# Two pairs of 512-column projection blocks in place of four blocks of 256, with their weights loaded from ScalarE's queue

## The chip, the core and the metric

The kernel runs on one core of one Trainium2 chip. The metric is the device time of one execution in microseconds. Before the change it is 2110.87 us, the median of three runs (2110.83 to 2110.98).

## The reference

One encoder layer over two sequences, a prompt of 512 tokens and a sample of 1024, width 1024, all float32. What matters here is the first stage, one wide projection whose result is cut into parts:

```python
proj = jnp.einsum('btd,de->bte', u, w_in) + b_in        # u = rmsnorm(x) * g
(na_q, na_k, na_v, gla_q, gla_k, gla_v, gla_g, lr_fwd, lr_bwd,
 gate_na, gate_gla) = jnp.split(proj, split_points, axis=-1)
na_o  = neighbourhood_attention(na_q, na_k, na_v, na_rpb)
gla_o = gla_bidirectional(gla_q, gla_k, gla_v, log_a_fwd, log_a_bwd)
gla_o = rmsnorm(gla_o, gla_norm_g) * silu(gla_g)
merged = sigmoid(gate_na) * (na_o @ w_br_na) + sigmoid(gate_gla) * (gla_o @ w_br_gla)
```

`gla_v`, `gla_g` and `na_v` are 512 columns wide each. After it come a squared-ReLU MLP and norms.

## The kernel before

Every float32 product is made from two float32r parts: an operand is split into a high part (ScalarE copies it to float32r) and a low part (VectorE subtracts), and three matmuls add hi*hi, hi*lo and lo*hi. The norm writes `u_hi` and `u_lo`, with d_model on the partitions, into SBUF, and they stay there for the whole projection.

The projection consists of units. A `dense_cm` unit gives 128 output columns for 512 tokens: the weights are stationary, 512 tokens stream, 24 matmuls. A `dense_tm` unit (token-major, L255) gives 256 output columns for 128 tokens: the tokens are stationary and 256 weight columns stream (`tm_half`, L244 to 253), also 24 matmuls. `gla_v` (second half, block 1), `na_v` (blocks 2 and 3) and `gla_g` (blocks 4 and 5) are token-major, 12 units each, in the order 4, then three units of `k1`, then 1, 5, 2, 3. (Block 0 is made earlier, while the norm runs.) Units 10 and 11 of a block are interleaved so that the block's first half of weights is free early.

The weights come through `Ring` (L32): tiles of 128x1024 are loaded by SyncE's queue into two raw buffers, split into three rotating pairs of buffers, and `fill` is called where a unit begins.

The result of a unit lies in one of three PSUM banks `psd` and is evacuated when `run_dense` (L343) calls `flush`, about 1.2 us of matmul after the unit's end. `out_tm` (L313) does it for token-major units: VectorE adds the bias (L316) into `sv`, one of two buffers `st`. Then, for blocks 4 and 5, ScalarE does a SiLU, GpSimd multiplies, and SyncE's queue stores it to `glag_d`; for blocks 2 and 3, ScalarE and VectorE split it (L153, L154) into `svr` or `svl`, one buffer each, and two DMAs store it to `nv_d`; for block 1 it is stored to `glav_d`.

Beside the units runs a side chain, the gated linear attention (`gla_all`, L554): `run_dense` counts the cost that a unit yields (0.325 for three matmuls of 256 columns, 0.65 for three of 512), and each time the count passes 3.9 it lets the side chain issue its next step. The side chain goes through levels: VectorE makes Q and K of a level (L633, L637) and what the next level needs (L646 to L649), TensorE multiplies them (L622), VectorE merges the product into `att` (L660). A step on TensorE takes two levels. There are three segments per head pair: 0P, 0S (two halves), 1P, 1S. Each ends with `kd` (L672, L694), an update (L703) and, after the last half, a scan on VectorE (L715, L716) that the output matmuls (L726, L727) wait for. Every engine executes its instructions in the order in which they were issued, so side chain and evacuation share VectorE in that order.

Of the kernel before, what the change touches and what calls it, by code (L numbers as in the profile page):

```python
# [31 lines left out]
class Ring:  # L32


    def __init__(self, nc, raw, rawtag, nraw, pool, tag, nslots, items):
        self.nc, self.raw, self.pool, self.items = nc, raw, pool, items
        self.rawtag, self.tag, self.nraw, self.nslots = rawtag, tag, nraw, nslots
        self.loaded, self.parts = [], []

    def load(self):  # L40
        i = len(self.loaded)
        t = self.raw.tile([128, 1024], F32, tag=self.rawtag, bufs=self.nraw, name=f"{self.tag}r{i}")
        self.nc.sync.dma_start(t, self.items[i])
        self.loaded.append(t)

    def split(self):
        i = len(self.parts)
        t = self.loaded[i]
        hi = self.pool.tile([128, 1024], F32R, tag=self.tag + "h", bufs=self.nslots, name=f"{self.tag}h{i}")
        lo = self.pool.tile([128, 1024], F32R, tag=self.tag + "l", bufs=self.nslots, name=f"{self.tag}l{i}")  # L50
        self.nc.scalar.activation(hi, t, AF.Copy)  # L51
        self.nc.vector.tensor_tensor(lo, t, hi.bitcast(F32), op=ALU.subtract)  # L52
        self.parts.append((hi, lo))

    def fill(self, live):
# [10 lines left out]
    def step(self, live):

        if len(self.parts) < min(len(self.items), live + self.nslots):
            if len(self.loaded) == len(self.parts):
                self.load()  # L70
            self.split()
            if len(self.loaded) < len(self.items):
                self.load()

    def get(self, i):
        return self.parts[i]
# [3 lines left out]
def tile_trunk(ctx: ExitStack, tc: tile.TileContext, d: dict, y: bass.AP):  # L80
    nc = tc.nc
# [25 lines left out]
    rngp = rnge.enter_context(tc.tile_pool(name="rng", bufs=1))  # L107
# [22 lines left out]
    def add_mv(b):  # L130
        add(f"mv{b}", d["wmv"][2 * b], d["wmv"][2 * b + 1])

    for n in ("q0", "k0", "q1"):
        add(n, d["wst"][ST[n]])
    add_mv(4)
    add("k1", d["wst"][3])
    add_mv(1)
    add_mv(5)
    add_mv(2)
    add_mv(3)  # L140
# [8 lines left out]
    ring = Ring(nc, raw, "wraw", 2, rngp, "w", 3, items)  # L149
# [8 lines left out]
    zero = cst.tile([128, 128], F32, name="zero")  # L158
    V.memset(zero, 0.0)
# [95 lines left out]
    def dense_tm(b, i, evac):  # L255


        wi = where[f"mv{b}"]

        def mm():  # L260
            if i == 0:
                ring.fill(wi)
            if b not in brow:
                load_brow(b)
            if i == 6 and TM.index(b) < 5:
                load_brow(TM[TM.index(b) + 1])
# [11 lines left out]
        return mm  # L278

# [142 lines left out]
    def norm_side():  # L422
# [11 lines left out]
        gkw = p0.tile([128, 512], F32, name="gkw")  # L434
# [30 lines left out]
        for i in range(1, 12):  # L465
# [20 lines left out]
    ns = norm_side()  # L486
    warm = ps("b")
# [336 lines left out]

    mid = []
# [387 lines left out]
    def wout(g, hook):  # L1213

        mh, ml = m_[g]
        for n in range(2):
            for kq in range(4):
# [5 lines left out]
                for t in range(6):  # L1223
# [78 lines left out]
    uraw, uhl, useq = {}, {}, []  # L1302
# [23 lines left out]
    def u_step(m):  # L1326


        if 0 < m <= 224:
# [19 lines left out]
    def up_all(side):  # L1349
# [62 lines left out]
        for p in range(33):  # L1412
            cu, pv = dict(p=p, g=p // 16, j=p % 16) if p < 32 else None, cu
            for pos in range(7):
                u = pv if pos == P4 else cu
                if u:
# [7 lines left out]
                    for k in range(4):  # L1424
# [3 lines left out]
                        T.matmul(u[b], wl[:, es], c[:, 0, k], start=False, stop=(k == 3), skip_group_check=True)  # L1428
                    ev(pos)
# [337 lines left out]
def _layout(x_prompt, x_sample, norm_mix_g, w_in, b_in, na_rpb, gk_fwd_w, gk_fwd_b, gk_bwd_w, gk_bwd_b,  # L1767
# [21 lines left out]
    d["wmv"] = c(np.stack([stat(w[h * 512:(h + 1) * 512, m:m + 256]) for m in mv for h in range(2)]))  # L1789
# [74 lines left out]
```

## Time and profile before

| | |
|---|---|
| median of three runs | 2110.87 us |
| profiled execution, its own time | 2112.74 us |
| its span, first to last instruction | 2110.8 us |
| TensorE busy | 2089.7 us (99%) |
| VectorE busy | 1318.2 us (62%) |
| ScalarE busy | 974.9 us (46%) |
| 256-column matmuls of L250 to L252 | 1440 in five blocks, 114.9 to 358.3 us |

TensorE's busy share counts each matmul from its start to its modelled end, and matmuls overlap, so the spacing between the starts of two neighbours is what one costs. The table says where time is spent over the whole run; what bounds one stretch is read from that stretch.

### The profile page before, as it was taken

Reading aid. Unit: us, or ns where it says so; the run is one execution under the profiler, and the core shown is the slowest. Engines: PE = TensorE matmul, PEld = TensorE weight load, DVE = VectorE, ACT = ScalarE, POOL = GpSimd, SP = SyncE. Lnnn points to the kernel's source line nnn. Section 1 sums busy time; section 2 is a strip of 40 time slices with the busy share of each in tenths; the row PEclk is TensorE's granted clock in tenths of the full one; section 3 lists DMA queues with packets and bytes.
Section 4 is the critical chain, followed back from the end, with each engine's and each line's share of the span. In section 5 each row is a group of like instructions: output and inputs, shape, how many; then the busy total and the mean of one; then the engine's idle time right before and its main releaser. Section 6 shows DMA issues by size and latency. Waiting matters only on the chain.

```text
span 2110.8 us, 32043 instructions
## 1 busy us (share of the span) xinstructions
PE 2089.7 (99%) x11964; PEld 1890.3 (90%) x11964; DVE 1318.2 (62%) x2428; ACT 974.9 (46%) x1914; POOL 64.5 (3%) x92
## 2 busy tenths in 40 slices
PE   9999999999999999999999999999999999999998
PEld 8899998888888888898898999999999888888887
DVE  7465875767346666465576777997887444443544
ACT  6532232333345555452353666676666333333442
POOL 1020100000000000000000000000000000000000
PEclk9999999999999999999999999999999999999999
DMA  6342334564386776466666566766876755454643
GB/s 212 116 147 86 97 112 140 126 170 91 111 246 202 217 217 198 149 212 226 245 215 250 174 165 173 228 202 197 267 234 176 264 200 186 157 170 162 220 170 110
DMA packets 256426, 381.86 MB, mean 181 GB/s; under 512 B 35856, under 2 KB 163856, under 8 KB 256272
## 3 DMA queue, kind: packets, MB, share of 16 engines
q1 hardware_dynamic: 256128, 379.56, 57.5%
q8 instruction: 94, 1.54, 0.3%
q14 instruction: 60, 0.49, 0.1%
q10 hardware_dynamic: 144, 0.26, 0.0%
HBM read 256.02 MB, written 123.73 MB: 180 GB/s over the span
## 4 chain that ended last, share of the span: by engine, by line
PE 80%; DVE 2%; ACT 1%; DMA 1%; issue 1%; SPq 0%; POOLq 0%; DVEq 0%; ACTq 0%
PE psd L225 6%; PE psd L227 6%; PE psd L226 6%; PE psa L1426 4%; PE psa L1428 4%; PE psa L1427 4%; PE psa L1581 2%; PE psa L1580 2%; PE psa L1582 2%; PE psb L1580 2%; PE psb L1581 2%; PE psb L1582 2%; PE psc L1581 2%; PE psc L1580 2%; PE psc L1582 2%; PE psb L1428 2%
## 5 line engine op out<-in xcount | busy, mean ns | idle before, releaser
L154 DVE TENSOR_TENSOR al<-al,ah 128x1024 fp32r<-128x1024 f32 x82 | 100.2, 1223 | 145.7 <-ACT ah L153 135.2
L153 ACT ACTIVATE ah<-al 128x1024 fp32r<-128x1024 f32 x82 | 86.6, 1057 | 225.2 <-DMA al<-ads 134.3
L225 PE MATMUL psd<-uhiS,wh 128*128 128x512 f32 x448 | 179.6, 401 | 0.8 <-ACT st L287 0.8
L227 PE MATMUL psd<-uhiS,wl 128*128 128x512 f32 x448 | 175.3, 391 | 0.0
L226 PE MATMUL psd<-uloS,wh 128*128 128x512 f32 x448 | 174.8, 390 | 0.0
L1426 PE MATMUL psa<-c,uwh 128*128 128x384 f32 x512 | 171.7, 335 | 0.8 <-DVE xb L1366 0.7
L1428 PE MATMUL psa<-c,uwl 128*128 128x384 f32 x512 | 171.0, 334 | 0.0
L1427 PE MATMUL psa<-c,uwh 128*128 128x384 f32 x512 | 171.0, 334 | 0.0
L1331 DVE TENSOR_TENSOR uwl<-ux,uwh 128x512 fp32r<-128x512 f32 x192 | 131.0, 687 | 58.7 <-ACT uwh L1347 57.6
L1347 ACT ACTIVATE uwh<-ux 128x512 fp32r<-128x512 f32 x192 | 120.0, 626 | 79.6 <-DVE ux L1341 66.3
L52 DVE TENSOR_TENSOR wl<-wr,wh 128x1024 fp32r<-128x1024 f32 x70 | 85.5, 1223 | 105.2 <-ACT wh L51 94.1
L51 ACT ACTIVATE wh<-wr 128x1024 fp32r<-128x1024 f32 x70 | 73.8, 1056 | 143.9 <-PE psc L1231 66.0
L225 PEld LDWEIGHTS psd<-uhiS,wh 128*128 128x128 f32 x448 | 84.2, 188 | 18.3 <-ACT st L287 1.2
L227 PEld LDWEIGHTS psd<-uhiS,wl 128*128 128x128 f32 x448 | 84.1, 188 | 18.2
L226 PEld LDWEIGHTS psd<-uloS,wh 128*128 128x128 f32 x448 | 84.3, 188 | 16.1
L1426 PEld LDWEIGHTS psa<-c,uwh 128*128 128x128 f32 x512 | 96.1, 188 | 1.5 <-DVE xb L1366 1.0
L1427 PEld LDWEIGHTS psa<-c,uwh 128*128 128x128 f32 x512 | 96.1, 188 | 0.0
L1428 PEld LDWEIGHTS psa<-c,uwl 128*128 128x128 f32 x512 | 96.1, 188 | 0.0
L250 PE MATMUL psd<-wh,uhiS 128*128 128x256 f32 x320 | 92.7, 290 | 0.8 <-DVE sv L316 0.8
L251 PE MATMUL psd<-wl,uhiS 128*128 128x256 f32 x320 | 90.9, 284 | 0.0
L252 PE MATMUL psd<-wh,uloS 128*128 128x256 f32 x320 | 90.8, 284 | 0.0
L225 PE MATMUL psd<-uhiP,wh 128*128 128x512 f32 x224 | 90.3, 403 | 0.0
(557 smaller groups left out, 5889.4 us busy)
## 6 DMA issues: line engine op xcount, KB each, us to landing
ux<-in_wup_dram SPq DMA_DIRECT2D x64, 512.0 KB
al<-ads SPq DMA_DIRECT2D x48, 512.0 KB
al<-ad SPq DMA_DIRECT2D x34, 512.0 KB
bq<-t_d SPq DMA_DIRECT2D x64, 256.0 KB
wr<-in_wst_dram SPq DMA_DIRECT2D x28, 512.0 KB
gate_d<-st SPq DMA_DIRECT2D x48, 256.0 KB
sg<-gate_d SPq DMA_DIRECT2D x32, 384.0 KB
ad<-xa SPq DMA_DIRECT2D x64, 192.0 KB
```

Source lines behind the costliest of these rows:

```text
L154: V.tensor_tensor(lo, src, hi.bitcast(F32), op=ALU.subtract)
L225: T.matmul(p, wh, xh[:, k, sl], start=(k == 0), stop=False)
L226: T.matmul(p, wh, xl[:, k, sl], start=False, stop=False)
L227: T.matmul(p, wl, xh[:, k, sl], start=False, stop=(k == 7))
L1331: V.tensor_tensor(lo, usrc.pop(m - 1), hi.bitcast(F32), op=ALU.subtract)
L1347: A.activation(uhl[m][0], usrc[m], AF.Copy)
L1426: T.matmul(u[b], wh[:, es], c[:, 0, k], start=(new and k == 0), stop=False, skip_group_check=True)
L1427: T.matmul(u[b], wh[:, es], c[:, 1, k], start=False, stop=False, skip_group_check=True)
L1428: T.matmul(u[b], wl[:, es], c[:, 0, k], start=False, stop=(k == 3), skip_group_check=True)
L1580: T.matmul(p, ah[:, jj], bh[:, cs], start=((new or last) and jj == 0), stop=False, skip_group_check=True)
L1581: T.matmul(p, ah[:, jj], bl[:, cs], start=False, stop=False, skip_group_check=True)
L1582: T.matmul(p, al[:, jj], bh[:, cs], start=False, stop=(kh == 1 and jj == 7), skip_group_check=True)
```

## The change

Blocks 4 and 5 become one pair, blocks 2 and 3 another. A unit of a pair (`dense_pair`) makes 512 columns for 128 tokens: 24 matmuls of 512 columns in place of 48 of 256. Its end evacuates both halves of the bank one after the other through the same `out_tm`. Units 0 and 1, and units 10 and 11, of a pair are interleaved. The order becomes `k1`, pair (4, 5), pair (2, 3), block 1. Units yield 0.68 per three matmuls.

The weights of a pair come as eight pieces of 128x512 from a new input array, loaded by `A.dma_start`, that is from ScalarE's queue, four of them in flight at the second pair and two at the first. A piece is split into one 128x1024 buffer, high half and low half. `Ring` has eight buffers without a fixed use and a free list. The first pair's pieces are split during `k1`, the second's during units 10 and 11 of the first pair and the first two units of its own. `pr` is a raw piece, `pw` a split one.

```diff
+    def alloc(self, dt, name):
+        s = self.free.pop(0)
+        return s, self.pool.tile([128, 1024], dt, tag=f"w{s}", name=name)
...
+    def pw_load(q, n=1, s=None):
...
+            if s is None:
+                t = stg2.tile([128, 512], F32, tag=("svr", "svl")[k % 2], bufs=1, name=f"pr{q}{k}")
...
+            A.dma_start(t, d["wpr"][q, k])
+    def pw_split(q):
...
+        s, x = ring.alloc(F32R, f"pw{q}{k}")
+        split_act(x[:, :512], x[:, 512:], t)
...
+    def pw_ahead(mm, q):
+        def run():
+            for n, cost in enumerate(mm()):
+                yield cost
+                if n % 4 == 3:
+                    pw_split(q)
+                    pw_load(q)
+    def dense_pair(q, i, evac, nxt=None):
+        def step(p, k, j):
+            x = pw[q]["parts"][k][1]
+            xh, xl = tok_ap(u_hi, k, j), tok_ap(u_lo, k, j)
+            T.matmul(p, xh, x[:, :512], start=(k == 0), stop=False)
+            T.matmul(p, xh, x[:, 512:], start=False, stop=False)
+            T.matmul(p, xl, x[:, :512], start=False, stop=(k == 7))
+        def end(p, j):
+            for e in range(2):
+                evac(p[:, e * 256:e * 256 + 256], PAIRS[q][e], j)
...
+            ii = (i, i + 1) if i in (0, 10) else (i,)
...
+                    step(p[j], k, j)
+                    yield 0.68
+                if i == 0:
+                    if k in (2, 4):
+                        pw_split(q)
...
+                if i == 10:
+                    ring.free.append(pw[q]["parts"][k][0])
+                    if nxt:
+                        nxt(k)
+    def next_pair(k):
+        if k == -1:
+            pw_load(1, 2)
+        elif k == 0:
+            pw_load(1, 2, 0)
+        elif k != 3:
+            pw_split(1)
+            if k in (1, 2, 6, 7):
+                pw_load(1)
+    def next_ring(k):
...
+        if k in (0, 1):
+            ring.load()
+        elif k in (5, 7):
+            ring.split()
-            r = stg2.tile([128, 4, 2, 64], F32R, tag=("svr", "svl")[i % 2], bufs=1, name=f"svr{uid[0]}")
+            r = stg2.tile([128, 4, 2, 64], F32R, tag=("svr", "svl")[(i + b) % 2], bufs=1, name=f"svr{uid[0]}")
...
-    mid += [dense_tm(4, i, out_tm) for i in range(12)]
-    for n_, dst, cb in (("k1", glak_d, 3),):
-        mid += [dense_cm(n_, seg, out_cm(dst, cb, 128, cb < 2)) for seg in range(3)]
-    for b in (1, 5, 2, 3):
-        mid += [dense_tm(b, i, out_tm) for i in range(12)]
+    pw_load(0, 2)
+    mid = [pw_ahead(dense_cm("k1", seg, out_cm(glak_d, 3, 128)), 0) for seg in range(3)]
+    for q, nxt in enumerate((next_pair, next_ring)):
+        mid += [dense_pair(q, i, out_tm, nxt) for i in (0, *range(2, 11))]
+    mid += [dense_tm(1, i, out_tm) for i in range(12)]
```

The rest of the diff moves the tile `zero` and `gkw` into buffers that are free later, gives the bias rows three buffers, and lets the MLP's first part take its buffers from the ring's free list. From the neighbourhood attention on, the order on every engine is the one of before.

The instructions move as follows. First VectorE in the sample's levels (0S). Before, in block 2, one evacuation (`sv` from `psd`, then `svr`) stands between two levels (Q, K, X, Y; `att0S` is the merge):

```order
L316 TENSOR_TENSOR sv_2968<-psd_2920,brow_2610 128x256
L154 TENSOR_TENSOR svr_2970<-sv_2968,svr_2970 128x4x64
L660 COPY_PREDICATED att0S<-msk,psa_2975 128x512
L660 COPY_PREDICATED att0S<-msk,psa_2976 128x512
L633 TENSOR_TENSOR Q0S_3015<-q0S_2332,Y0S_2334 128x2x32x8
L637 TENSOR_TENSOR K0S_3017<-k0S_2333,X0S_2769 128x2x32x8
L646 TENSOR_TENSOR X0S_2769<-X0S_2769,Y0S_2334 128x32x8
L647 TENSOR_TENSOR X0S_2769<-X0S_2769,Y0S_2334 128x32x8
L649 TENSOR_TENSOR Y0S_2334<-Y0S_2334 128x2x32x8
L316 TENSOR_TENSOR sv_3038<-psd_2964,brow_2610 128x256
L154 TENSOR_TENSOR svr_3040<-sv_3038,svr_3040 128x4x64
```

Now, at the end of the first two units of pair (2, 3), four evacuations stand in a row ahead of the merge and the next K:

```order
L405 TENSOR_TENSOR sv_2239<-psd_2104,brow_1742 128x256
L146 TENSOR_TENSOR svr_2241<-sv_2239,svr_2241 128x4x64
L405 TENSOR_TENSOR sv_2246<-psd_2104,brow_2190 128x256
L146 TENSOR_TENSOR svr_2248<-sv_2246,svr_2248 128x4x64
L405 TENSOR_TENSOR sv_2260<-psd_2140,brow_1742 128x256
L146 TENSOR_TENSOR svr_2262<-sv_2260,svr_2262 128x4x64
L405 TENSOR_TENSOR sv_2267<-psd_2140,brow_2190 128x256
L146 TENSOR_TENSOR svr_2269<-sv_2267,svr_2269 128x4x64
L752 COPY_PREDICATED att0S<-msk,psa_2208 128x512
L752 COPY_PREDICATED att0S<-msk,psa_2209 128x512
L725 TENSOR_TENSOR Q0S_2285<-q0S_1394,Y0S_1396 128x2x4x64
L729 TENSOR_TENSOR K0S_2287<-k0S_1395,X0S_1705 128x2x4x64
```

Four evacuations, each a sum and a split, stand where there was one, and K of the level behind them comes after all four.

Second VectorE in the prompt's levels (0P). Before, in block 4, single evacuations stand between merges and levels:

```order
L316 TENSOR_TENSOR sv_1493<-psd_1443,brow_436 128x256
L660 COPY_PREDICATED att0P<-msk,psa_1429 128x512
L660 COPY_PREDICATED att0P<-msk,psa_1430 128x512
L316 TENSOR_TENSOR sv_1526<-psd_1480,brow_436 128x256
L633 TENSOR_TENSOR Q0P_1531<-q0P_1263,Y0P_1265 128x2x64x4
L637 TENSOR_TENSOR K0P_1533<-k0P_1264,X0P_1408 128x2x64x4
L646 TENSOR_TENSOR X0P_1408<-X0P_1408,Y0P_1265 128x64x4
L647 TENSOR_TENSOR X0P_1408<-X0P_1408,Y0P_1265 128x64x4
L649 TENSOR_TENSOR Y0P_1265<-Y0P_1265 128x2x64x4
L660 COPY_PREDICATED att0P<-msk,psa_1556 128x512
L660 COPY_PREDICATED att0P<-msk,psa_1557 128x512
```

Now the first two units of pair (4, 5) are evacuated in one go, four times into the two buffers `st`:

```order
L729 TENSOR_TENSOR K0P_1467<-k0P_1232,X0P_1326 128x2x32x8
L738 TENSOR_TENSOR X0P_1326<-X0P_1326,Y0P_1233 128x32x8
L739 TENSOR_TENSOR X0P_1326<-X0P_1326,Y0P_1233 128x32x8
L741 TENSOR_TENSOR Y0P_1233<-Y0P_1233 128x2x32x8
L405 TENSOR_TENSOR sv_1475<-psd_1364,brow_433 128x256
L405 TENSOR_TENSOR sv_1480<-psd_1364,brow_435 128x256
L405 TENSOR_TENSOR sv_1492<-psd_1371,brow_433 128x256
L405 TENSOR_TENSOR sv_1497<-psd_1371,brow_435 128x256
L752 COPY_PREDICATED att0P<-msk,psa_1444 128x512
L752 COPY_PREDICATED att0P<-msk,psa_1445 128x512
L725 TENSOR_TENSOR Q0P_1513<-q0P_1231,Y0P_1233 128x2x16x16
L729 TENSOR_TENSOR K0P_1515<-k0P_1232,X0P_1326 128x2x16x16
```

The third `sv` takes the buffer of the first, whose path through ScalarE, GpSimd and the store must have ended; the next Q and K stand behind it.

Third ScalarE at the change from the first pair to the second. Before, at the start of block 5, its queue holds two splits and then SiLUs:

```order
L51 ACTIVATE wh_2308<-wr_1716 128x1024
L51 ACTIVATE wh_2350<-wr_1890 128x1024
L332 ACTIVATE sv_2395<-sv_2395 128x256
L332 ACTIVATE sv_2463<-sv_2463 128x256
L332 ACTIVATE sv_2492<-sv_2492 128x256
L332 ACTIVATE sv_2523<-sv_2523 128x256
L332 ACTIVATE sv_2591<-sv_2591 128x256
L332 ACTIVATE sv_2622<-sv_2622 128x256
```

Now, in units 10 and 11 of pair (4, 5), DMA issues stand between the splits:

```order
L282 DMA pr_1974<-in_wpr_dram 128x512 x2
L145 ACTIVATE pw_1983<-pr_1897 128x512
L282 DMA pr_1986<-in_wpr_dram 128x512
L145 ACTIVATE pw_2020<-pr_1899 128x512
L282 DMA pr_2023<-in_wpr_dram 128x512
L145 ACTIVATE pw_2044<-pr_1974 128x512
L145 ACTIVATE pw_2062<-pr_1974 128x512
L145 ACTIVATE pw_2078<-pr_1986 128x512
L282 DMA pr_2081<-in_wpr_dram 128x512
L421 ACTIVATE sv_2089<-sv_2089 128x256
L421 ACTIVATE sv_2094<-sv_2094 128x256
```

Each DMA that reuses a raw buffer waits in ScalarE's queue until VectorE has made the low part from it.

## Rows read from the trace of the kernel before

**Rows 1.** Page, part 1: busy us (share) xinstructions of each engine.

```profile
PE 2089.7 (99%) x11964; PEld 1890.3 (90%) x11964; DVE 1318.2 (62%) x2428; ACT 974.9 (46%) x1914; POOL 64.5 (3%) x92
```

**Rows 2.** Stretches: PE, PEld, DVE, ACT, POOL busy us, granted clock, DMA share, GB/s.

```profile
115.00:211.00 96.00, 95.92 (x785) 91.17 (x785) 55.62 (x110) 25.40 (x61) 14.56 (x18) 1.00 0.35 115
211.00:331.00 120.00, 114.09 (x1031) 109.99 (x1027) 97.86 (x192) 32.60 (x72) 11.01 (x12) 1.00 0.33 106
...
140.00:150.00 10.00, 10.00 (x99) 9.75 (x98) 9.86 (x19) 1.40 (x4) 3.28 (x3) 1.00 0.45 145
...
330.00:340.00 10.00, 8.81 (x60) 8.67 (x61) 3.38 (x9) 2.61 (x11) 0.81 (x1) 0.83 0.27 79
```

**Rows 3.** Timeline of TensorE, token-major units: start us, duration us, line, tiles.

```profile
120.18 0.28 PE L250 MATMUL psd<-wh,uhiP 128*128 128x256 f32 x1
120.30 0.28 PE L251 MATMUL psd<-wl,uhiP 128*128 128x256 f32 x1
```

**Rows 4.** Timeline of TensorE, column-major units of 512.

```profile
71.05 0.39 PE L226 MATMUL psd<-uloS,wh 128*128 128x512 f32 x1
...
71.73 0.39 PE L226 MATMUL psd<-uloS,wh 128*128 128x512 f32 x1
```

**Rows 5.** Waits of TensorE, 100 to 700 us: total, times, longest.

```profile
PE psa L727 <- DVE stt0S L716: 2.6, 1, 2.6
PE psa L622 <- DVE K0S L637: 1.8, 2, 1.1
```

**Rows 6.** Timeline of TensorE, the side chain's steps that begin and end segment 0S.

```profile
210.23 0.50 PE L611 MATMUL psa<-qkh,two 64*128 64x512 f32 x2
...
242.24 2.06 PE L622 MATMUL psa<-Q0S,K0S 64*128 64x128 f32 x32
...
331.19 0.46 PE L727 MATMUL psa<-stt0S,qd0S 128*128 128x128 f32 x2 [2.58 <-DVE stt0S L716]
```

**Rows 7.** Timeline of VectorE in block 2: evacuation, merge, level, evacuation.

```profile
282.41 0.42 DVE L316 TENSOR_TENSOR sv<-psd,brow 128x256 f32<-128x256 f32 x1
283.36 0.43 DVE L154 TENSOR_TENSOR svr<-sv,svr 128x256 fp32r<-128x256 f32 x1 [0.53 <-ACT svr L153]
283.70 1.35 DVE L660 COPY_PREDICATED att0S<-msk,psa 128x512 f32<-128x512 uint8 x2
...
287.05 0.69 DVE L649 TENSOR_TENSOR Y0S<-Y0S 128x512 f32<-128x512 f32 x1
287.66 0.42 DVE L316 TENSOR_TENSOR sv<-psd,brow 128x256 f32<-128x256 f32 x1
```

**Rows 8.** Groups of VectorE, 211 to 332 us: busy, mean ns | idle before, releasers.

```profile
L316 DVE TENSOR_TENSOR sv<-psd,brow 128x256 f32<-128x256 f32 x31 | 13.0, 419 | 3.5 <-PE psd L252 2.5 <-POOL sv L334 0.9
...
L52 DVE TENSOR_TENSOR wl<-wr,wh 128x1024 fp32r<-128x1024 f32 x6 | 7.3, 1222 | 2.4 <-ACT wh L51 2.4
L154 DVE TENSOR_TENSOR svr<-sv,svr 128x256 fp32r<-128x256 f32 x16 | 6.8, 426 | 9.7 <-ACT svr L153 9.7
...
L154 DVE TENSOR_TENSOR qkl<-qk,qkh 128x512 fp32r<-128x512 f32 x2 | 1.4, 693 | 4.6 <-ACT qkh L153 4.6
```

**Rows 9.** Waits that a store's buffer ended, 100 to 480 us.

```profile
DVE sv L316 <- DMA glag_d<-sv: 7.3, 2, 3.8
...
ACT svr L153 <- DMA nv_d<-svr: 4.4, 1, 4.4
```

**Rows 10.** SyncE's queue: two stores.

```profile
109.32 0.80 SPq L541 DMA_DIRECT2D la_d<-zz  x2
...
120.79 0.32 SPq L335 DMA_DIRECT2D glag_d<-sv  x1
```

**Rows 11.** Timeline of VectorE: the instructions that waited for these stores; the start of 0P.

```profile
112.16 1.41 DVE L531 TENSOR_SCALAR zz<-psa,gkb 128x512 f32<-128x512 f32 x2 [2.56 <-DMA la_d<-zz]
...
124.99 0.42 DVE L316 TENSOR_TENSOR sv<-psd,brow 128x256 f32<-128x256 f32 x1 [3.47 <-DMA glag_d<-sv]
...
130.14 0.68 DVE L597 TENSOR_TENSOR qk<-q0P,k0P 128x512 f32<-128x512 f32 x1
```

**Rows 12.** Timeline of ScalarE: the split of 128x512.

```profile
130.85 0.63 ACT L153 ACTIVATE qkh<-qk 128x512 fp32r<-128x512 f32 x1 [0.18 <-DVE qk L597]
```

More of the change, by code (lines that the diff above doesn't have):

```diff
@@ L64, in fill @@
                 return
[L66 to L73, printed above, removed]
     def get(self, i):
-        return self.parts[i]
+        return self.parts[i][2:]
 @with_exitstack
@@ L128, in add @@
         items.extend(aps)
-    def add_mv(b):
-        add(f"mv{b}", d["wmv"][2 * b], d["wmv"][2 * b + 1])
-    for n in ("q0", "k0", "q1"):
+    for n in ("q0", "k0", "q1", "k1"):
         add(n, d["wst"][ST[n]])
[L135 to L140, printed above, removed]
+    add("mv1", d["wmv"][0], d["wmv"][1])
     for i in range(8):
@@ L148, in tile_trunk @@
         add(f"out{g}", *[d["wout"][i] for i in range(8)])
-    ring = Ring(nc, raw, "wraw", 2, rngp, "w", 3, items)
+    ring = Ring(nc, raw, 8, items)
+    ring.limit = where["mv1"]
     def split_act(hi, lo, src):
@@ L260, in mm @@
         def mm():
-            if i == 0:
+            if i == 4:
                 ring.fill(wi)
[L263 to L266, printed above, removed]
             if i == 11:
@@ L278, in dense_tm @@
         return mm
+    PAIRS = ((4, 5), (2, 3))
+    pw = [dict(n=0, raw=[], parts={}) for _ in PAIRS]
+    def pw_load(q, n=1, s=None):
+        w = pw[q]
+        if s is not None:
+            b, x = ring.alloc(F32, f"pr{q}{w['n']}")
+        for e in range(n):
+            k = w["n"]
+            if s is None:
+                t = stg2.tile([128, 512], F32, tag=("svr", "svl")[k % 2], bufs=1, name=f"pr{q}{k}")
+                w["raw"].append((t, None))
+            else:
+                t = x[:, e * 512:e * 512 + 512]
+                w["raw"].append((t, b if e == n - 1 else None))
+            A.dma_start(t, d["wpr"][q, k])
+            w["n"] += 1
@@ new lines, in pw_split @@
+    def pw_split(q):
+        w = pw[q]
+        k = len(w["parts"])
+        t, b = w["raw"].pop(0)
+        s, x = ring.alloc(F32R, f"pw{q}{k}")
+        split_act(x[:, :512], x[:, 512:], t)
+        w["parts"][k] = s, x
+        if b is not None:
+            ring.free.append(b)
+    def pw_ahead(mm, q):
[5 more added lines that the diff above has]
+                    pw_load(q)
+        return run
@@ new lines, in dense_pair, with mm @@
+    def dense_pair(q, i, evac, nxt=None):
[8 more added lines that the diff above has]
+                evac(p[:, e * 256:e * 256 + 256], PAIRS[q][e], j)
+        def mm():
+            if i == 0 and q == 0:
+                ring.release(where["k1"] + 1)
+            if i == 9 and nxt:
+                nxt(-1)
+            ii = (i, i + 1) if i in (0, 10) else (i,)
+            p = {}
+            for k in range(8):
+                for j in ii:
+                    if k == 0:
+                        if j == 1:
+                            flush()
+                        p[j] = ps("d")
+                    step(p[j], k, j)
+                    yield 0.68
+                    if k == 7:
+                        done.append(lambda j=j: end(p[j], j))
+                if i == 0:
+                    if k in (2, 4):
+                        pw_split(q)
+                    if k == 4:
+                        for b in PAIRS[q]:
+                            if b not in brow:
+                                load_brow(b)
+                if i == 6 and k == 0:
+                    load_brow(PAIRS[1][0] if q == 0 else 1)
+                if i == 10:
+                    ring.free.append(pw[q]["parts"][k][0])
+                    if nxt:
+                        nxt(k)
+        return mm
@@ L280, in out_cm @@
+    def next_pair(k):
[8 more added lines that the diff above has]
+    def next_ring(k):
+        ring.limit = len(items)
+        if k in (0, 1):
+            ring.load()
+        elif k in (5, 7):
+            ring.split()
+            if k == 7:
+                ring.load()
     def out_cm(dst, cb, row, scale=False):
@@ L433, in norm_side @@
         SP.dma_start(gkb, d["gkb"])
-        gkw = p0.tile([128, 512], F32, name="gkw")
         xn = {}
@@ L486, in tile_trunk @@
     ns = norm_side()
+    zero = p0.tile([128, 4, 32], F32, tag="lrt", bufs=4, name="zero").rearrange("p a b -> p (a b)")
+    V.memset(zero, 0.0)
     warm = ps("b")
@@ L1234, in wout @@
                         V.tensor_tensor(hs, acc[t], hs, op=ALU.add)
+                ring.release(wi + 1)
                 hook(n * 4 + kq)
@@ L1310, in u_load @@
             for e in es:
-                x = raw.tile([128, 1024], F32, tag="wraw", bufs=2, name=f"ux{p}{e}") if p % 2 == 0 else tmp(f"ux{p}{e}")
+                s, x = ring.alloc(F32, f"ux{p}{e}") if p % 2 == 0 else (None, tmp(f"ux{p}{e}"))
+                uslot.setdefault(p, []).append(s)
                 SP.dma_start(x, d["wup"][p % 16 * 2 + e])
@@ L1334, in u_step @@
                 uraw.pop(p)
+                ring.free += [s for s in uslot.pop(p) if s is not None]
                 u_load(p + 2)
@@ L1343, in u_step @@
             if m % 2 == 0:
-                uhl["t"] = [rngp.tile([128, 1024], F32R, tag=f"w{c}", bufs=3, name=f"uw{c}{m}") for c in "hl"]
+                uslot["w", m + 1], uhl["t"] = zip(*[ring.alloc(F32R, f"uw{c}{m}") for c in "hl"])
             sl = slice(m % 2 * 512, m % 2 * 512 + 512)
@@ L1428, in up_all @@
                         T.matmul(u[b], wl[:, es], c[:, 0, k], start=False, stop=(k == 3), skip_group_check=True)
+                    ring.free += uslot.pop(("w", n), ())
                     ev(pos)
```

43 lines of the change are left out of this document (22 added, 21 removed).

## The prediction

> **What bounds the kernel now.** I read the busy shares first: TensorE 99%, VectorE 62% [rows 1]. That makes TensorE the bound of the run, but the change touches only 115 to 358 us, so I read that stretch alone. There VectorE is busy for 55.6 of 96 us up to 211 us and for 97.9 of 120 us from there to 331 us, and in the second piece TensorE is idle for 120.0 - 114.1 = 5.9 us [rows 2]. The waits of TensorE say who ended that idle time: VectorE's scan (2.6 us) and the K of a level (1.8 us) are the largest [rows 5]. So in the sample's segment 0S, from its first matmuls at 210.23 us to the output matmul released at 331.19 us [rows 6], 121.0 us, TensorE and VectorE are close to a tie, and VectorE is a little late at the end. Elsewhere in the stretch TensorE waits for almost nothing.
>
> **What goes: half of 1152 matmuls.** Matmuls of 256 columns start 0.12 us apart [rows 3], those of 512 columns 0.227 us apart [rows 4] (0.68 us from one L226 to the next, three matmuls). Four blocks of 288 are 1152 x 0.120 = 138.2 us, two pairs of 288 are 576 x 0.2267 = 130.6 us: -7.7 us. The fixed part of a matmul, 2 x 0.120 - 0.2267 = 13 ns, is all there is to win.
>
> [...]
>
> **What is added on VectorE and ScalarE.** The four blocks' splits were 8 of 1.22 us on VectorE and become 16 of 128x512, for which `qkl` stands with 0.69 us [rows 8] (ScalarE 0.63 us each [rows 12]): +1.2 us on VectorE. Evacuations stay 48, each of 256 columns. What moves is where they stand. Before, the 24 that also split (blocks 2 and 3) lay beside the second half of 0S and its scan, and the first half of 0S lay beside blocks 1 and 5, whose evacuation is one instruction. Now pair (2, 3) lies beside nearly all of 0S.
>
> One such evacuation holds VectorE for 283.70 - 282.41 = 1.29 us, 0.53 of it idle for ScalarE; a level (merge to `Y`) holds it for 287.66 - 283.70 = 3.96 us [rows 7]. A TensorE step takes two levels. It costs TensorE 2.06 us [rows 6] and 7.8 us of counted dense cost: before 72 matmuls, 8.64 us, together 10.8; now 7.8 us of pair, together 9.96. VectorE needs 7.92 for the levels and 3.87 for three evacuations before, 11.8; now 7.8/5.44 x 2 x 1.29 = 3.7, so 11.6. VectorE was short by 1.0 us per step in block 2 and is short by 1.7 us in pair (2, 3), for five steps where there were three.
>
> **Sum over 0S.** VectorE's 120.8 us there contain evacuations and splits of dense weights: 15 plain sums at 0.34 (spacing), 16 with a split at 0.76 and their 9.7 us of waiting, six ring splits at 1.15 and 2.4 us, 3.5 us of other waits: 39.8 us [rows 8]. `qkl` waited 4.6 us, of which some 1.4 stays. The rest, 120.8 - 39.8 - 3.2 = 77.8 us, is the side chain. Counted in the new order between the same two points, VectorE has 7 piece splits (0.65 each), 5 plain sums, 24 sums with split at 1.29, 2 ring splits: 4.6 + 1.7 + 31.0 + 2.3 = 39.6 us. So 117.4 us if it never waits for a buffer.
>
> It will wait. In both interleaved unit pairs (0 and 1, 10 and 11) four evacuations become due within 0.7 us, and the third takes a buffer of the first two. For blocks 4 and 5 that is `st`: sum, SiLU, multiply, store; such waits were 3.8 and 3.5 us [rows 9]. For blocks 2 and 3 it is `svr`/`svl`, behind two stores; the one wait of that kind was 4.4 us [rows 9]. A store lands 112.16 - 110.12 = 2.0 us after its issue ended, or 124.99 - 121.11 = 3.9 us beside loads [rows 10, 11]. In 0S that hits three times (end of the first pair, start and end of the second): none to 3.3 us each, so 0 to 10 us; I take 6, 2 each, as `svr`'s DMAs start while the sums go on. VectorE then needs 123.4 us.
>
> TensorE's own work in the same piece: before 121.0 - 6.0 of waits = 115.0, of which 753 dense matmuls (counted in the order) are 90.4 and the side chain 24.6. Now 321 of pairs, 72.8, 78 of block 1, 9.4, and 24.6: 106.8. VectorE with 123.4 sets the end of the piece, with 123.4 - 121.0 = +2.4 us. Dense work that is no longer done inside it is done outside: the total falls by 7.7, the piece's own by 8.2, so the outside rises by 0.5.
>
> **The prompt's levels.** Two more waits come at the start of pair (4, 5). `qk` of 0P, made from 130.14 us before [rows 11], now stands on VectorE behind the fifth piece split. Two raw buffers, a load of 2.0 to 3.9 us (no row shows one alone, so I take the two stores above as bounds), 0.63 on ScalarE, 0.69 on VectorE, 0.35 to issue: the fifth is done at 130 to 132.5 us, and TensorE, which wants `qkl` at 131.4, waits 0 to 2.2 us; I take 1.0. Then units 0 and 1 are evacuated, the third sum waits for the store of the first (0 to 4.5 us), and K of the next level stands behind it; TensorE has a slack of about 1 us per step there (9.96 against 7.92 + 1.0). I take 3.0 of 0 to 4.1.
>
> **The rest.** After the 2.6 us wait the clock was granted at 0.83 for 10 us [rows 2], which cost 1.7 us. With a wait at the same place, and longer ones before, I leave it: 0, bounds -1.7 and +3. `mv1`, loaded and split in units 10 and 11 of the second pair, is in the 123.4. The other edits (`zero`, `gkw`, bias rows, the MLP's buffers) change no order from the neighbourhood attention on and lie beside work at the start: 0, bounds -0.3 and +0.3.
>
> Sum: +2.4 + 0.5 + 1.0 + 3.0 = +6.9 us. It is made against the profiled execution (span 2110.8, own time 2112.74, so 1.9 us lie around the span; the median of the runs is 1.87 below that execution). The change is inside the span, so I add it to the median: 2110.87 + 6.9 = 2117.8.
>
> **Rivals.** *TensorE stays the bound.* The burst costs VectorE nothing that reaches TensorE, because a K is made up to one step ahead and three PSUM banks hold results. For it: at 140 to 150 us, in block 4, VectorE was busy for 9.9 of 10 us and TensorE for all 10 [rows 2]. Against it: the tie in 0S. Time: -7.7, 2103.2; if the 6.0 us of waits and the slow clock go too, 2095.5. *It cancels.* VectorE sets the end of 0S, but stores land early enough: 117.4 - 121.0 + 0.5 = -3.1, and 1 to 4 us at the prompt: 2109 to 2112, I say 2110. *The pieces come late.* Everything of the forecast and, in front of both pairs, TensorE waits for a split piece, since ScalarE issues a load only when VectorE has emptied the buffer and then does nothing else while it waits. Price: a cycle of two pieces gets 2.0 us longer if a load takes 4.5 us and not 2.5, and there are three cycles ahead of 0P: +6, 2124; it decides where a load takes over 3.5 us. For it: loads in this stretch share the queues with the side chain's. Against it: the second pair has four in flight. *The change does not do what it says:* the order shows 576 fewer matmuls, so only a spacing over 0.24 us would undo it, and rows 4 exclude that.
>
> **Chances.** Forecast (2113 to 2122) 0.42, TensorE stays the bound 0.20, it cancels 0.23, pieces late 0.15. Some 0.2%, 4.2 us, is what a measurement of this kernel can tell from no change: below 2106.7 faster, above 2115.1 slower. The first rival is faster, the second the same, and of the forecast 0.03 falls in the same: 0.20, 0.26, 0.54. The forecast's own range is 2113 to 2122; as both signs hold much of the chance, the range for 8 in 10 goes from 2103 (most of the first rival at its plain -7.7) to 2126 (pieces late and a slow clock).
>
> **What would show it.** Right: matmuls of L310 to L312 start 0.227 us apart; TensorE's waits for K0S (now L729) sum to over 10 us in 0S, the longest behind the first two units of pair (2, 3); VectorE waits 2 to 4 us for the stores of `glag_d` at those of pair (4, 5), and TensorE for K0P behind it; VectorE over 90% busy or waiting for ScalarE through 0S. Wrong: TensorE idle in 115 to 360 us stays near 6 us; or it waits for `pw` at pair starts; or a third `sv` finds its buffer free.

## The result, and the profile after

The changed kernel takes 2126.62 us (median of four runs, 2126.47 to 2127.79), the kernel before 2110.93 beside it: ratio 1.0073, 95% interval [1.0061, 1.0086], +15.7 us. The forecast was 2117.8, with 2126 as the upper end. The direction was right, the size less than half of what came. The profiled execution is the one of 2126.47 us, span 2124.7.

The busy shares after, to be held against [rows 1]: 576 fewer matmuls, and TensorE busy for the same time.

```profile
PE 2089.0 (98%) x11388; PEld 1862.8 (88%) x11388; DVE 1316.2 (62%) x2436; ACT 975.6 (46%) x1922; POOL 62.3 (3%) x92
```

The stretches (columns as in [rows 2]); the second is segment 0S, now 211.20 to 341.71 us:

```profile
115.00:211.00 96.00, 91.40 (x501) 75.34 (x499) 55.99 (x111) 28.57 (x73) 18.20 (x23) 0.98 0.35 112
211.00:342.00 131.00, 113.66 (x685) 94.22 (x684) 99.43 (x205) 34.44 (x78) 4.70 (x8) 0.93 0.33 108
342.00:375.00 33.00, 33.00 (x285) 32.48 (x284) 11.77 (x31) 8.14 (x37) 4.59 (x6) 1.00 0.43 134
130.00:140.00 10.00, 7.11 (x36) 5.05 (x35) 7.53 (x14) 2.87 (x5) 0.00 (x0) 0.83 0.43 131
230.00:240.00 10.00, 7.83 (x51) 6.37 (x50) 9.83 (x19) 0.00 (x0) 0.00 (x0) 0.83 0.09 30
250.00:260.00 10.00, 7.31 (x30) 6.02 (x31) 6.20 (x13) 3.33 (x11) 0.00 (x0) 0.54 0.21 65
300.00:310.00 10.00, 7.01 (x43) 5.84 (x42) 6.07 (x13) 4.02 (x12) 0.00 (x0) 0.83 0.16 53
```

Two things are to be seen. TensorE is idle for 17.3 us of 0S, where [rows 2] had 5.9, and for 4.6 us ahead of it, where there was 0.1. And the granted clock is low in four places, not one. What that costs is estimated as busy time times what the clock lacks of 1.00, taken microsecond by microsecond, since a row of ten mixes idle time with busy time: 1.7, 1.6, 3.2 and 1.6 us in the four places. (Nine matmuls of 512 columns at 0.50, 255.29 to 258.71 us, start 0.43 us apart; nine at 1.00, 260.05 to 261.89 us, 0.23.) From 115 us to the first column-major matmul behind the stretch that is 8.0 us after and 1.7 before.

Who ended TensorE's waits, 115 to 380 us (columns as in [rows 5]):

```profile
PE psa L714 <- DVE K0S L729: 11.0, 3, 5.9
PE psa L703 <- issue: 2.6, 1, 2.6
PE psa L714 <- DVE K0P L729: 1.7, 1, 1.7
```

Each of the four low stretches begins inside one of these or within about 2 us behind it: the start of 0P (2.6 us, low from 136 us) and the three K0S (2.2, 5.9, 3.0 us, low from 235, 249 and 303 us). (At the start of 0P the view names no releaser, only "issue"; what TensorE multiplies there, `qkh`, is ready at 134.10 us, and it starts at 134.20.) The longest stands behind the first two units of pair (2, 3). VectorE there, in the order of issue listed above (columns as in [rows 7]):

```profile
242.20 0.43 DVE L146 TENSOR_TENSOR svr<-sv,svr 128x256 fp32r<-128x256 f32 x1 [0.54 <-ACT svr L145]
242.54 0.42 DVE L405 TENSOR_TENSOR sv<-psd,brow 128x256 f32<-128x256 f32 x1
243.50 0.42 DVE L146 TENSOR_TENSOR svr<-sv,svr 128x256 fp32r<-128x256 f32 x1 [0.54 <-ACT svr L145]
243.84 0.41 DVE L405 TENSOR_TENSOR sv<-psd,brow 128x256 f32<-128x256 f32 x1
248.47 0.42 DVE L146 TENSOR_TENSOR svr<-sv,svr 128x256 fp32r<-128x256 f32 x1 [4.21 <-ACT svr L145]
248.81 0.42 DVE L405 TENSOR_TENSOR sv<-psd,brow 128x256 f32<-128x256 f32 x1
249.71 0.42 DVE L146 TENSOR_TENSOR svr<-sv,svr 128x256 fp32r<-128x256 f32 x1 [0.48 <-ACT svr L145]
250.05 1.32 DVE L752 COPY_PREDICATED att0S<-msk,psa 128x512 f32<-128x512 uint8 x2
251.26 0.68 DVE L725 TENSOR_TENSOR Q0S<-q0S,Y0S 128x512 f32<-128x512 f32 x1
251.86 0.69 DVE L729 TENSOR_TENSOR K0S<-k0S,X0S 128x512 f32<-128x512 f32 x1
...
256.38 0.42 DVE L405 TENSOR_TENSOR sv<-psd,brow 128x256 f32<-128x256 f32 x1 [2.32 <-PE psd L312]
```

ScalarE says what the third `svr` waited for, and TensorE what the K held up:

```profile
248.02 0.42 ACT L145 ACTIVATE svr<-sv 128x256 fp32r<-128x256 f32 x1 [4.55 <-DMA nv_d<-svr]
```

```profile
252.69 2.08 PE L714 MATMUL psa<-Q0S,K0S 64*128 64x128 f32 x16 [5.87 <-DVE K0S L729]
```

Read as one chain: two evacuations fill `svr` and `svl`; the third high part, which by `(i + b) % 2` wants the buffer that the second has just filled, waits 4.55 us until its store to `nv_d` is done; VectorE waits behind it; K, made only at 251.86, is wanted by TensorE from 246.8; TensorE stands, then runs at a granted clock of 0.50 until 259 us (0.54 in the row of 250 to 260 us); and VectorE, with its backlog done, waits 2.3 us, until 256.38, for the slow TensorE. In that chain the two engines' losses add. They do not hide each other.

### The profile page after: what moved, and what is told of

Read it like the earlier page. It is cut to its first block, busy times and chain, and to the rows that moved or that the text cites. A ratio compares the mean times of both kernels' runs of the same rounds, so it can differ in the third digit from the quotient of the medians.

```text
span 2124.7 us, 30926 instructions
## 1 busy us (share of the span) xinstructions
PE 2089.0 (98%) x11388; PEld 1862.8 (88%) x11388; DVE 1316.2 (62%) x2436; ACT 975.6 (46%) x1922; POOL 62.3 (3%) x92
## 4 chain that ended last, share of the span: by engine, by line
PE 89%; DVE 5%; DMA 2%; ACT 2%; issue 1%; POOL 0%; SPq 0%; ACTq 0%; POOLq 0%; DVEq 0%
PE psd L215 7%; PE psd L217 7%; PE psd L216 7%; PE psa L1520 4%; PE psa L1522 4%; PE psa L1521 4%; PE psa L1677 2%; PE psa L1676 2%; PE psa L1675 2%; PE psb L1677 2%; PE psb L1675 2%; PE psb L1676 2%; PE psc L1677 2%; PE psc L1676 2%; PE psc L1675 2%; PE psc L1077 2%
## 5 line engine op out<-in xcount | busy, mean ns | idle before, releaser
L54 DVE TENSOR_TENSOR wl<-wr,wh 128x1024 fp32r<-128x1024 f32 x62 | 75.8, 1224 | 118.0 <-ACT wh L53 95.7
L53 ACT ACTIVATE wh<-wr 128x1024 fp32r<-128x1024 f32 x62 | 65.3, 1055 | 128.3 <-PE psc L1322 64.4
L217 PE MATMUL psd<-uhiP,wl 128*128 128x512 f32 x224 | 87.7, 391 | 0.0
L216 PE MATMUL psd<-uloP,wh 128*128 128x512 f32 x224 | 87.4, 390 | 0.0
L1522 PE MATMUL psb<-c,uwl 128*128 128x384 f32 x256 | 85.5, 334 | 0.0
```

Of the source, the lines that this page charges most:

```text
L216: T.matmul(p, wh, xl[:, k, sl], start=False, stop=False)
L217: T.matmul(p, wl, xh[:, k, sl], start=False, stop=(k == 7))
```

## The experiments

Theory A: the bursts of evacuations wait for store buffers, K stands behind them, and the low clock behind TensorE's waits is paid. Theory B, the rival: VectorE's sum in 0S, with its idle inside each evacuation, sets the end wherever an evacuation stands. A second rival: piece loads from ScalarE's queue. Each kernel starts from the changed one unless said otherwise; times are medians of 4 to 11 runs, ratios stand against the kernel before on the same chip. The kernel before took 2110.69 to 2111.70 us on these chips, so a difference between two runs on different chips is good to about 1 us.

**Clock alone.**

```
+ keep(FILL.get((i, l, x), 0))      # ahead of four score/diag groups
+ T.matmul(ps("b"), u_hi["P"][:, 0, :128], u_hi["P"][:, 0, :512], ...)   # n times
```

> 57 matmuls of 512 columns that compute nothing for the output stand in TensorE's program ahead of the four waits for qk and K0S that were 2.2 us or longer (11, 9, 25 and 12 of them, 0.227 us each: 2.5, 2.0, 5.7, 2.7 us), so that TensorE works while it would wait. Theory A (the waits are followed by a stretch at half clock, and that stretch is paid): the granted clock stays at 1.00 behind those places, and of the 8.0 us that the low clock cost between 115 and 376 us most comes back: 2119 to 2122. Theory B (VectorE sets the end of the segment, the low clock only slows an engine that has slack there): the clock stays up, later waits for K0S grow by the same, 2125 to 2127.

2123.22 us, ratio 1.0055 [1.0042, 1.0067]. The K0S waits fall from 11.0 to 1.4 us by design, and the clock holds, as the ten-microsecond rows at the same places show:

```profile
250.00:260.00 10.00, 8.71 (x50) 7.31 (x51) 7.41 (x18) 4.59 (x13) 0.00 (x0) 1.00 0.26 87
230.00:240.00 10.00, 10.00 (x66) 7.91 (x65) 9.83 (x19) 0.00 (x0) 0.00 (x0) 1.00 0.03 10
300.00:310.00 10.00, 9.95 (x56) 7.96 (x55) 7.97 (x20) 3.95 (x11) 0.00 (x0) 1.00 0.29 96
```

The time lies 3.4 us below the changed kernel, a little above what A expected. The low clock costs 3.4 us (same sum) where it cost 8.0, since new low stretches came behind other waits (156 to 160 and 327 to 331 us). So of 4.6 us of clock given back, 3.4 reach the end. Most of the rest went into waits: the 57 matmuls (12.9 us) and the idle time that is left (10.0) are 1.0 us more than the idle time of the changed kernel (22.0). The clock is a real term, worth three quarters or more of what the rows show. It is not the larger part of the 15.7.

**Evacuations spread, first try.**

```
- done.append(lambda j=j: end(p[j], j))
+ for e in range(2): (done if j == 10 else late).append(...)   # one per 2.6 us of dense cost
- tag=("svr", "svl")[(i + b) % 2]
+ tag=("svr", "svl")[b % 2]
```

> The 48 evacuations of the pairs no longer become due four at a time: one is issued per 2.6 us of dense cost (only unit 10's two go at once), and of blocks 2 and 3 each has its own store buffer. Theory A (the burst waits for its store buffers, K stands behind it, and the clock falls behind that wait): the 4 us waits of ScalarE's svr for the nv_d stores go, TensorE's wait of 5.9 us at the first K0S behind the pair's start goes with the 3.5 us of low clock behind it, and part of the others: 2114 to 2119. Theory B (the sum of VectorE's work in the segment sets its end, wherever an evacuation stands): waits are spread, not gone, 2124 to 2128.

2125.30 us, ratio 1.0066 [1.0053, 1.008]: by that it would be theory B. The waits say otherwise. K0S falls from 11.0 to 5.3 us, and a new wait appears, in front of units 10 and 11, which want two PSUM banks while the evacuations still lag:

```profile
310.31 0.76 PE L310 MATMUL psd<-pw,uhiS 128*128 128x512 f32 x1 [5.52 <-DVE sv L406]
```

A pace of 2.6 us per evacuation is 5.2 per unit, and a unit is done every 5.44: the lag of a burst shrinks by only 0.24 us per unit. The run is inconclusive as it was built; it is taken up again below.

**The first pieces earlier.**

```
- pw_load(0, 2)                      # ahead of k1
+ pw_load(0, 2)                      # ahead of run_dense(q0[1:] + k0 + q1, ...)
```

> The first two piece loads of pair (4,5) are issued one stage earlier (ahead of the q0, k0, q1 units), the rest follows as before. Theory A (the late pieces hold VectorE and so qk at 131 us): the 2.6 us wait at 134 us falls under 0.5 and the clock behind it stays up (1.7 us): 2121 to 2124. Theory B (the loads behind the first two are late as before, beside the loads of 0P): same wait, 2125 to 2128.

2122.97 us, ratio 1.0059 [1.0047, 1.0072], 3.65 us below the changed kernel; two of the five runs took 2125.3, so the time alone would not decide. The trace does: the wait at 134 us is gone (0.2 us are left, for `qkl`). So the piece that came late held VectorE, and `qk` stood behind it: in the changed kernel ScalarE issued that load at 122.78 us and could split it only at 129.13.

```profile
122.78 0.33 ACTq L282 DMA_DIRECT2D pr<-in_wpr_dram  x1
...
129.13 0.63 ACT L145 ACTIVATE pw<-pr 128x512 fp32r<-128x512 f32 x1 [4.71 <-DMA pr<-in_wpr_dram]
```

**512 columns or twice 256.**

```
- T.matmul(p, xh, x[:, :512], ...)         # and two more
+ for c in (0, 256): T.matmul(p[:, c:c + 256], xh, x[:, c:c + 256], ...)   # and two more
```

> Each matmul of a pair with 512 columns is two of 256 columns (1152 in place of 576), all else as in the changed kernel. If TensorE's time in the pairs were all on the path, it is 576 x 13 ns = 7.7 us slower, 2134. If VectorE and its waits set the segment 0S, the 321 matmuls that lie there (4.3 us) are hidden in TensorE's waits and only the rest shows: 2129 to 2131. If a matmul of 512 columns gained nothing over two of 256: 2126 to 2127.

2129.42 us, ratio 1.0087 [1.0074, 1.0101], +2.8 us on the changed kernel (+2.0 if each is held against the kernel before beside it), within the second case by its number. The trace does not bear out the split that was expected: 0S is 2.2 us longer (132.7), and up to its start only 0.3 us are lost, since the low clock at the start of 0P (1.7 us) does not come. TensorE's idle time falls from 22.0 to 19.2 us, so some of the 6.7 us that wide matmuls save (see below) lies in its waits. How much stays open: the intervals of the two ratios overlap.

**Both evacuations of a unit side by side.**

```
- for e in range(2): evac(...)             # sum, high, low; sum, high, low
+ rest = [evac(..., True) for e in range(2)]   # sum, sum
+ for n in range(2): [r(n) for r in rest]      # high, high; low, low and the stores
- tag=("svr", "svl")[(i + b) % 2]
+ tag=("svr", "svl")[b % 2]
```

> The two evacuations of a unit go side by side: both sums first, then both high parts on ScalarE, then both low parts on VectorE, so that VectorE no longer stands idle 0.5 us for ScalarE in each (24 times, 18.2 us in all with the long one). The stores and their buffers stay two. Theory B (VectorE's sum, with the idle inside each evacuation, sets the end of 0S): some 9 us of it go, K0S waits fall by about that, 2117 to 2120. Theory A (the burst at a pair's start waits for its store buffers and K stands behind it): the wait at the start of pair (2,3) stays at 4 us or more with the low clock behind it, 2121 to 2125.

2118.06 us, ratio 1.003 [1.0019, 1.0041]: 8.6 us below the changed kernel, by an edit that takes no work away. VectorE's wait for ScalarE in 0S, after and in this run:

```profile
DVE svr L146 <- ACT svr L145: 18.2, 24, 4.2
```

```profile
DVE svr L419 <- ACT svr L417: 9.7, 14, 3.9
```

8.5 us less, and 0S is 122.0 us long in place of 130.5. Theory B is right in this much: the idle inside an evacuation is on the path. It is not all of it: the long K0S wait stays, as A expected, and the low clock costs 7.9 us as before:

```profile
PE psa L727 <- DVE K0S L742: 7.8, 3, 5.0
```

The edit also gives each block its own store buffer, so that the third evacuation wants the buffer of the first and not of the second. That alone moved little: its high part waits 4.57 us for a store, where it waited 4.55.

**The same, with the units spread.**

```
+ (done if j == 10 else late).append(lambda j=j: end(p[j], j))   # one unit per 4.2 us of dense cost
```

> As pairsum, and the evacuation of a unit starts 4.2 us of dense cost behind the one before it at the earliest (unit 10's at once), so that a burst of two units no longer falls on buffers whose stores are under way; a PSUM bank is kept at most 5.4 us longer, which three banks allow. Theory A: ScalarE's waits for nv_d stores (8.5 us) go, K0S waits (11.0 us) go under 4, the clock behind them stays up: 2112 to 2117, some 5 us below pairsum. Theory B: as pairsum within 2 us.

2109.78 us, ratio 0.9992 [0.9983, 1.0001]: 8.3 us below pairsum, level with the kernel before, lower than A expected. The low clock costs 3.4 us in place of 7.9, and 0S is 116.9 us long:

```profile
PE psa L734 <- DVE K0S L749: 3.9, 3, 2.2
```

```profile
ACT svr L417 <- DMA nv_d<-svr: 5.4, 3, 2.6
```

So the waits for the stores are shorter, not gone as A had it (9.9 us in pairsum). The work of every engine is that of pairsum; only the moment of an evacuation differs. That is theory A. The 5.5 us wait of the first try ahead of units 10 and 11 is gone too; since this run changes both the pace and the order of evacuations, it is not shown which of the two spoiled the first try.

**Low parts on GpSimd.**

```
- split_act(r[:, :, 0], r[:, :, 1], t3)
+ A.activation(r[:, :, 0], t3, AF.Copy)
+ G.tensor_tensor(r[:, :, 1], t3, r[:, :, 0].bitcast(F32), op=ALU.subtract)
```

> The low parts of blocks 2 and 3 (24 subtractions) are made by GpSimd, all else as in the changed kernel: VectorE loses 24 x 0.34 us and the 0.5 us in which it waits for ScalarE ahead of each, some 20 us, and the 4.2 us stand behind the store, since then ScalarE waits there alone. Theory B (VectorE's work and idle set 0S): K0S waits fall from 11.0 to under 3, 2114 to 2118. Theory A in its narrow form (the store buffer itself must come free): the third high part still waits, but no K stands behind it on VectorE, so the wait at K0S goes too; what tells them apart is which of the three K0S waits stays. If GpSimd takes over 2 us for one, the stores are late and PSUM banks come free late: 2122 or more.

2114.34 us, ratio 1.0014 [1.0006, 1.0023]: 12.3 us below the changed kernel, 0S 118.4 us. ScalarE still waits, and longer, for the store buffers (26.0 us against 8.5), but no K stands behind it, and the waits for K0S fall to 2.2 us, with one of 2.4 us for a Q:

```profile
ACT svr L412 <- DMA nv_d<-svr: 26.0, 6, 6.1
```

```profile
PE psa L715 <- DVE Q0S L726: 2.4, 1, 2.4
PE psa L715 <- DVE K0S L730: 2.2, 1, 2.2
```

So it is not the store that costs time; it is what is queued behind the instruction that waits for it. The run also takes work off VectorE, as theory B would have it, so it does not tell the two theories apart. What it gained is idle time of TensorE (22.0 to 11.6 us); the low clock costs 8.3 us, as much as in the changed kernel.

**Put together.** The first also splits `mv1` one step earlier:

```
best1:  unitpace + early, and  elif k in (5, 7): ring.split()  ->  k in (4, 6)
ue:     unitpace + early
uep:    ue + low parts on GpSimd
```

> As unitpace, with the first two piece loads a stage earlier (as in the run of that name) and block 1's two weight splits one step earlier in units 10 and 11 of the second pair. If the waits at 134 us, at the pairs' starts and at block 1's start are separate causes, they add: some 4 and 2 to 3 us below unitpace, 2106 to 2112, about the kernel before. If each wait that goes only lets TensorE run into the next one: 2113 to 2118.

2110.75 us, ratio 0.9996 [0.9987, 1.0005]. Inside the first range by its number, but not for its reason: nothing below unitpace, so the gains did not add. With `mv1`'s splits a step earlier the low part of the first stands in VectorE's queue ahead of the scan and not behind its first steps, and waits there for ScalarE; what is queued behind it is late, up to the sum that frees a bank for block 1:

```profile
304.16 1.23 DVE L54 TENSOR_TENSOR wl<-wr,wh 128x1024 fp32r<-128x1024 f32 x1 [5.31 <-ACT wh L53]
```

```profile
320.80 0.58 PE L239 MATMUL psd<-wh,uhiP 128*128 128x256 f32 x1 [3.84 <-DVE sv L408]
```

> unitpace with the first two piece loads one stage earlier, and block 1's weight splits where they are in the changed kernel. If the wait at 134 us and the low clock behind it (2.4 + 1.7 us in unitpace) add to the rest, as they did alone (about 4 us in the run early): 2104 to 2107, below the kernel before. If 0S takes the time back: 2109 to 2111.

2105.78 us, ratio 0.9978 [0.9969, 0.9987]: without that edit the two gains add, 4.0 us below unitpace, and the result lies below the kernel before.

> As ue, with the 24 low parts of blocks 2 and 3 made by GpSimd (0.90 us each in the run pool_lo) in place of VectorE (0.34 spaced). If VectorE still sets 0S in ue, its 24 x 0.34 us and the waits for ScalarE ahead of them come off K0S: 2100 to 2105. If TensorE or the store buffers set it by then: within 1.5 us of ue, or above it, since a buffer is stored 0.6 us later.

2101.43 us, ratio 0.9958 [0.9944, 0.9972]: below both kernels. TensorE is at full clock throughout the stretch, with 7.1 us idle:

```profile
115.00:205.00 90.00, 89.49 (x502) 73.88 (x502) 56.92 (x110) 28.11 (x73) 18.42 (x24) 1.00 0.35 116
205.00:317.00 112.00, 105.45 (x678) 87.97 (x675) 97.24 (x181) 33.86 (x77) 25.32 (x31) 1.00 0.38 122
```

**The rival queue.**

```
- A.dma_start(t, d["wpr"][q, k])
+ SP.dma_start(t, d["wpr"][q, k])
```

> The pieces of both pairs are loaded from SyncE's queue, not ScalarE's, all else as in the changed kernel. Theory A and B (burst, ping-pong and clock): ScalarE waits for the same pieces, within 2 us of the changed kernel, 2124 to 2128, or slower, since an issue that waits for its buffer now holds SyncE's stores. Rival (the queue on ScalarE makes the pieces late: 10.6 us of its waits for pr, and 16 issues of 0.33 us): 2118 to 2122.

2129.06 us, ratio 1.0087 [1.0073, 1.0101]. The four runs lie at 2126.6, 2127.0, 2131.1 and 2131.2, so level with the changed kernel or slower, not faster. In the trace, of the run of 2131.1, TensorE's wait at the start of 0P is 3.8 us in place of 2.6, and ScalarE's waits for pieces are longer, not shorter (10.6 us in the changed kernel):

```profile
ACT pw L145 <- DMA pr<-in_wpr_dram: 20.1, 8, 5.9
```

Late pieces are thus not a matter of ScalarE's queue as against SyncE's, and that rival falls. A queue without other work was not tried.

**The kernel before, with the same relief.** Its `split_act(r...)` changed as in pool_lo, nothing else.

> The kernel before with the 24 low parts of blocks 2 and 3 made by GpSimd, all else as it was. What it tells: how much of uep (2101.4) comes from relieving VectorE alone. If the kernel before was nearly free of VectorE (6.2 us of TensorE waits and 1.7 of low clock between 115 and 359 us), it can win at most those: 2104 to 2109, and the pairs themselves are worth 3 to 7 us once nothing waits. If the pairs give nothing: 2101 to 2103.

2103.15 us, ratio 0.9964 [0.9952, 0.9977], 1 us below what was expected. Between 115 and 349 us TensorE waits for almost nothing and keeps its clock:

```profile
115.00:211.00 96.00, 95.92 (x793) 91.23 (x791) 55.95 (x110) 25.05 (x61) 14.44 (x18) 1.00 0.36 116
211.00:324.00 113.00, 112.14 (x1021) 109.24 (x1020) 95.66 (x178) 32.51 (x72) 24.49 (x28) 1.00 0.35 110
```

Nearly all of uep's gain is thus to be had by two lines and without the pairs. Between uep and this run lie 1.7 us, on different chips and with overlapping intervals, so it stays open whether the pairs are worth anything at all. In the stretch itself they gave nothing: uep's first column-major matmul behind it starts at 351.25 us, here at 349.47. uep is ahead only in what follows, which is 3.7 us shorter there; 1.3 us of that is a wait for K1S that uep does not have, and the rest is not explained.

## Why the prediction was right or wrong

*TensorE's term, -7.7: nearly right.* Over 517 successive starts the matmuls of L310 to L312 are 0.2281 us apart, not 0.2267, and those of the kernel before 0.1199 (1383 starts): 576 x 0.2281 - 1152 x 0.1199 = -6.7 us.

*Clock, 0 between -1.7 and +3: the term that failed most plainly.* It is +6.3 (8.0 against 1.7 us), twice its upper bound. The forecast had seen one wait of 2.6 us with 1.7 us of low clock behind it [rows 2, 5] and itself predicted over 10 us of further waits, yet left the term where it was. That step failed: waits were priced by their own length and the low clock behind them at nothing. Priced as that row shows, three more such waits are 5 us. The run fill shows that some 3.4 of 4.6 us come back when the clock holds.

*0S, +2.4 with 6 us of waits: mechanism right, sized by a rule that did not hold.* The places were right: K0S waits sum to 11.0 us ("over 10"), the longest behind the first two units of pair (2, 3). Buffer waits were about as assumed: 5.5 us beyond the 0.53 per evacuation (18.2 - 24 x 0.53), and 0.8 for `glag_d`. But the sum treated VectorE as busy or waiting for a store through 123.4 us and TensorE as hidden behind it. In the trace 0S takes 130.5 us, since VectorE also waits for TensorE and for pieces:

```profile
DVE sv L405 <- PE psd L312: 4.6, 3, 2.3
DVE pw L146 <- ACT pw L145: 2.8, 2, 1.8
```

Those 7.4 us are about the 7.1 by which 0S was too short (smaller differences, some 3 us each way, cancel). Seen from TensorE the same 0S has 11.5 us more of idle time and 6.3 more of low clock, and some 8 us less of matmuls; so this term and the clock's overlap, and are not to be added. Where two engines wait for each other in turn, the larger of two sums is a lower bound, not the time.

*Start of 0P, +1.0 of 0 to 2.2: too small.* TensorE waited 2.6 and 0.2 us. The bound rested on loads of 2.0 to 3.9 us, from two stores [rows 10, 11]; the piece issued at 122.78 was there only some 6 us later, on a queue of its own, beside 3.28 MB that SyncE's queue moved between 115 and 135 us. That is the rival "the pieces come late", which was to decide above 3.5 us. It came together with the forecast and not in its place: alone the run early takes back 3.65 us.

*Third `sv` of pair (4, 5), +3.0 of 0 to 4.1: right in kind.* VectorE waits 3.0 us for `glag_d` at 155.45, and TensorE 1.7 for the K0P behind it:

```profile
155.45 0.97 DVE L405 TENSOR_TENSOR sv<-psd,brow 128x256 f32<-128x256 f32 x2 [3.01 <-DMA glag_d<-sv]
```

*Sums.* In "What is added" TensorE's step is 8.64 + 2.06 = 10.7 and 7.8 + 2.06 = 9.86, not 10.8 and 9.96; VectorE is then short by 1.1 and 1.8 us. No term of the sum moves by more than that 0.1. The counts of matmuls in 0S (753; 321 and 78) were exact.

*The balance.* Stretch 115 us to the first column-major matmul behind it: idle 22.0 - 6.2 = +15.8, clock +6.3, matmuls -6.7, together +15.4; measured +17.2 (375.87 against 358.68 us). 1.8 us stay unassigned. At the end of the span +13.9 are left: 3.3 us come back later, where the kernel before still waited for K1S and K1P (1.9 us) and the changed one does not. (The medians are 15.7 apart; the profiled execution of the kernel before lies 1.9 above its median.)

*Chances.* The rivals were weighed as alternatives, each with its own time. Late pieces, bursts and the clock are one chain, and their prices add: 0.15 for 2124 and an end at 2126 was too little room above.

## What to carry to other kernels

When a change makes several results fall due at once, look at which buffer the third one wants and at what is queued behind it on the same engine; spreading them and doing the two evacuations of a unit side by side were together worth 17 us here, without taking any work away. Price each expected wait of the matmul engine with the low clock behind it, from a row that shows one. And before a change that buys a few nanoseconds per matmul, ask whether the neighbour engine is the one to relieve: two lines that use GpSimd gave the kernel before 8 us, nearly what the whole rebuilt version gave.

## What the runs showed of the hardware

In the changed kernel a granted clock of 0.50 (236 to 238 us) came with a wait of only 2.2 us, which ended at 235 us. Its length alone did not decide: in the same kernel no low clock followed the wait of 1.7 us at 159 us, in pairsum one of 2.0 us there cost 1.7 us (160 to 162 us at 0.50), and in uep a wait of 2.2 us, at 228 us, cost nothing (1.00 throughout).

GpSimd's subtraction of 128x256 took 0.90 us in pool_lo, where VectorE's took 0.43 [rows 7, 8]; for work that no engine waits for, it paid all the same, 12.3 us:

```profile
L413 POOL TENSOR_TENSOR svr<-sv,svr 128x256 fp32r<-128x256 f32 x24 | 21.1, 897 | 76.6 <-ACT svr L412 76.6
```

Beside it VectorE took longer in some places: in uep four of the twelve K0S took 1.22 to 1.24 us, where all twelve of the changed kernel took 0.68 or 0.69, and each of the four ran while GpSimd subtracted:

```profile
255.12 2.13 POOL L419 TENSOR_TENSOR svr<-sv,svr 128x256 fp32r<-128x256 f32 x2 [6.38 <-ACT svr L417]
```

```profile
255.43 1.24 DVE L750 TENSOR_TENSOR K0S<-k0S,X0S 128x512 f32<-128x512 f32 x1
```
